# Spreading a kernel's weight transfers over more of the run, and splitting one more input weight ahead

## The chip, the cores and the metric

The kernel runs on one core of a Trainium2 chip. Its time is the device time of one execution in microseconds (us). A core has five engines that run their own queues of instructions and wait for each other by semaphores: TensorE (PE, matrix products), VectorE (DVE), ScalarE (ACT), GpSimd (POOL) and SyncE (SP). Here POOL and SP issue the DMA transfers: SP loads, POOL most stores and everything that adds while it moves. All transfers run on 16 DMA engines.

## What is computed

One decoder layer on x of 2048 rows by 1024 columns, in fp32:

```python
h = x * (1.0 + sc1) + sh1
z = h @ w_in[l]
gate_b, gate_c, v_conv, v_pool = jnp.split(z, [CONV_CH, 2 * CONV_CH, 3 * CONV_CH], axis=-1)
y_conv = gate_b * _short_conv(gate_c * v_conv, conv_w[l])
y_pool = _multiscale_pool(v_pool, w_pool[l], pool_scale[l])
mix = jnp.concatenate([y_conv, y_pool], axis=-1) @ w_out[l]
x = _layer_norm(DEEPNORM_ALPHA * x + (1.0 + g1) * mix, ln1_g[l], ln1_b[l])
h = x * (1.0 + sc2) + sh2
f = jnp.square(jax.nn.relu(h @ w_mlp_in[l])) @ w_mlp_out[l]
x = _layer_norm(DEEPNORM_ALPHA * x + (1.0 + g2) * f, ln2_g[l], ln2_b[l])
```

w_in is 1024 x 2048, w_out 1024 x 1024, w_mlp_in 1024 x 4096, w_mlp_out 4096 x 1024; the shifts, scales and gates come from a conditioning vector and w_ada.

## The kernel before

**Products.** The rows are worked in two blocks of 1024. Each fp32 operand is split into a high half (fp32r, a cast on ACT, line 145) and a low half (the rest, a subtraction on DVE, line 146); a product of 128 x 128 by 128 x 512 is then three matmuls, high by high, high by low and low by high (`mm3`, lines 152, 153 and 154). The large products use seven products of halved blocks in place of eight (a Strassen scheme), so that sums of weight blocks and of operand blocks are needed. `seven` (line 626) runs one such set of seven: a product takes a pair (high, low) of a weight from the list `made`, or splits one, runs 8 `mm3` (24 matmuls), and splits the next weight behind itself. The split weights live in six tiles `w` of 128 x 1024, that is three pairs. The names of the operand blocks in their order are 11, 12, s2, s1, s3, s4, 22 for the weights and "11", "21", "2", "1", "3", "22", "4" for the inputs.

**Stages on PE, in order.** Block 0: input projection (`in_proj_0`, to about 190 us), output projection (`out_proj`, to about 270), first map of the MLP (`first_map`, eight groups of seven products, 448 `mm3`, to about 580). Block 1: input projection (`in_proj_1`, four groups of seven products, 224 `mm3`, to about 735), output projection (112 `mm3`, to about 819), first map (448 `mm3`, to about 1131). Then the second map (`down`, 26 products, to 1701) and the last normalisation. During the first map of a block, each group's results are squared on ACT, added in many combinations on DVE (`sums`, quarter tiles of 128 x 256) and stored to the DRAM tensor `usum` by POOL (line 1108). The last group of block 0 leaves these sums `owed`; `flush` hands them out inside block 1's input projection.

**The weight transfers.** The second map needs sums of blocks of w_mlp_out. They are not worked on DVE: `sums_down` (line 1187) is a list of 20 sums of 4 parts each, 80 DMA transfers of 512 KB from DRAM to DRAM into `wsum`, all issued by POOL at line 1191; 40 of them copy, 40 add into what is there. They are handed out one at a time: once the generator `sums_down()` is in the list `beside_products`, each `mm3` counts one beat, and at the beats of the set `W_BEATS` (line 31) one transfer is issued; `behind` lets POOL wait for that `mm3`'s last matmul. POOL's queue is in order, so what stands behind a transfer there (stores of `usum`, of `msum`, loads of x) waits as well. Before the change the list is filled after block 0's first map, so that beat 1 is the first `mm3` of block 1's input projection: beats 56 to 206 (26 of them) lie in that projection, beats 207 to 359, with its end and the output projection, have none, and 54 transfers follow from beat 360 on, every seventh beat, in block 1's first map; the last at beat 731 of 784.

**The turn from block 0 to block 1.** Ahead of product 5 of the last group of block 0's first map, `prepare` (line 716) is called: it starts the generator of the projection's weights (`summed_weights`, line 620: an SP load into one of five tiles `r`), splits the first weight, and makes the inputs "11", "21" and "2" (`inputs`, line 694: two SP loads each; the first two kinds are scaled and shifted on ACT, "2" is only split). `in_proj_1` (line 724) then runs group 0; behind its first product it splits the second weight, flushes one owed stage and makes input "1"; behind the second product it splits the third weight, adds, flushes the rest and makes input "3"; and so on. At the end of a projection its results are mixed and stored to `msum` (lines 418 and 420, POOL), and the output projection's operands are loaded from `msum`, `gout` and `wosum` by SP (lines 923, 931 and 941). In the last group the pooling (line 334) and the convolution (lines 398 to 400) run between the last products; `keep` (line 731; the copy is line 733) empties PE's banks on ACT.

**What sets the order.** The source gives each instruction its engine and a priority (its place in the program). A planner lays down each engine's queue when the kernel is built, by its own estimate of when an operand or a free tile is there; so an engine's order can differ from the source's, PE's too, and an edit at one place can move instructions at others. On the chip every queue runs in the order so laid down.

Of the kernel before, what the change touches and what calls it, by code (L numbers as in the profile page):

```python
# [27 lines left out]
WINDOWS = (2, 4, 8, 16)  # L28
HALO = 16
Q = 256  # L30
W_BEATS = {*range(56, 210, 6), *range(360, 776, 7)}
QUARTERS = slice(0, 256), slice(256, 512)

SLOTS = 26
# [73 lines left out]
def tile_hybrid_layer(ctx: ExitStack, tc: tile.TileContext, opening, xT, x, wada, win,  # L108
# [26 lines left out]
    def t_r():  # L135
        return mk(big, [P, T], F32, "r", 5)

    def t_ps():
        return mk(pp, [P, H], F32, "ps", 8)
# [11 lines left out]
    def mm3(ps, whi, wlo, xhi, xlo, first, last, goes_on=False):  # L151
# [4 lines left out]
        if beside_products:  # L156
            beats[0] += 1
            if beats[0] in W_BEATS:
                with behind(done.ins):
# [186 lines left out]
    def parts(src, t=t_h):  # L346
        hi, lo = t(), t()
        split(src, hi, lo)
        return hi, lo
# [239 lines left out]
    ORDER = (("11", "11"), ("12", "21"), ("s2", "2"), ("s1", "1"), ("s3", "3"), ("s4", "22"), ("22", "4"))  # L589
# [33 lines left out]
            nc.sync.dma_start(r, src[i] if i in RAW else sums[i - 4])  # L623
            yield r

    def seven(ready, B, first_w=None):
        made = [first_w] if first_w else []

        def product(i, banks, new):
            hi, lo = made.pop() if made else parts(next(ready), t_w)  # L630
            for p in range(2):
                if new:
                    banks[p] = t_ps()
                for k in range(4):
                    bh, bl = B[ORDER[i][1], k // 2]
                    ks = slice((k % 2) * H, (k % 2) * H + H)
                    cs = slice(p * H + k * P, p * H + k * P + P)
                    mm3(banks[p], hi[:, cs], lo[:, cs], bh[:, ks], bl[:, ks], new and k == 0, k == 3,
                        not new)
            for r in ready:  # L640
                made.append(parts(r, t_w))
                break

        return product
# [49 lines left out]
    def inputs(X, key):  # L694
        for q in range(2):
            r = t_r()
            X[key, q] = hi, lo = t_h(), t_h()
            if len(key) == 1:
                src, hs = xsum[(int(key) + 1) % 2], halves[int(key) % 4 > 0 and int(key) < 3]
                k = 2 * q  # L700
            else:
                k, hs = 4 * int(key[0]) - 4 + 2 * q, halves[int(key[1]) - 1]
                src = xT
            nc.sync.dma_start(r.rearrange("p (a n) -> p a n", a=2),
                              src[k : k + 2, :, hs].rearrange("a p n -> p a n"))
            if len(key) == 1:
                split(r, hi, lo)
                continue
            for dst in (hi, r):
                for a, cs in enumerate(halves):  # L710
                    nc.scalar.activation(dst[:, cs], r[:, cs], AF.Identity,
                                         bias=mod[:, 2 * (k + a) + SH1 : 2 * (k + a) + SH1 + 1],
                                         scale=mod[:, 2 * (k + a) + SC1 : 2 * (k + a) + SC1 + 1])
            tt(lo, r, hi.bitcast(F32), ALU.subtract)

    def prepare():
        X = {}
        W = summed_weights(wins[0], winsum, (0, 1, 5, 4, 6, 7, 3))
        first_w = parts(next(W), t_w)
        for i in range(3):  # L720
            inputs(X, ORDER[i][1])
        return X, W, first_w

    def in_proj_1(X, W, first_w):
        mixed = []
        ops = Operands(mixed)

        def cut(rows_, h):
            return [r[:, o + h * H : o + h * H + H] for r, o in rows_]

        def keep(dst, banks):
            for p in range(2):
                nc.scalar.copy(dst[p], banks[p])  # L733

        def add(dst, banks):
            for p in range(2):
                tt(dst[p], dst[p], banks[p], ALU.add)

        def group(j):
            x_, y_, z_ = {}, {}, {}  # L740
            ready = W if j == 0 else block_weights(wins[j])
            product = seven(ready, X, None if j else first_w)
            v, u = t_o(WW), t_o(WW)
            values = (v, HALO), (u, 2)
            product(0, x_, True)
            keep(cut(values, 0), x_)
            if owed:
                flush(1)
            nc.vector.tensor_copy(v[:, :HALO], vhalo[:, j, :])
            nc.vector.tensor_copy(u[:, :2], uhalo[:, j, :])  # L750
            if j == 0:
                inputs(X, ORDER[3][1])
            product(1, y_, True)
            add(cut(values, 0), y_)
            flush()
            if j == 0:
                inputs(X, ORDER[4][1])
            yield
            gc, gb = t_o(), t_o()
            gates = (gc, 0), (gb, 0)  # L760
            last = j == NG - 1
            product(2, x_, False)
            keep(cut(values, 1), x_)
            if j == 0:
                inputs(X, ORDER[5][1])
            product(3, z_, True)
            keep(cut(gates, 1), z_)
            if j == 0:
                inputs(X, ORDER[6][1])
            if last:  # L770
                ops.begin(0)
            yield
            product(4, x_, False)
            add(cut(gates, 1), x_)
            if last:
                ops.begin(1)
            product(5, z_, False)
            add(cut(values, 1), z_)
            if last:
                ops.weights(0, 1)  # L780
                pt = pool_mid(1, j, v)
            product(6, x_, False)
            keep(cut(gates, 0), x_)
            if last:
                ops.weights(1, 1)
                ops.second(0)
            yield
            if not last:
                pt = pool_mid(1, j, v)
            y = gc  # L790
            for hs in halves if last else [slice(0, T)]:
                w = hs.stop - hs.start
                tt(u[:, 2 + hs.start : 2 + hs.stop], u[:, 2 + hs.start : 2 + hs.stop], gc[:, hs], ALU.mult)
                conv(j, u[:, hs.start : hs.stop + 2], y[:, hs], w)
                tt(y[:, hs], y[:, hs], gb[:, hs], ALU.mult)
                if last and hs.start == 0:
                    mixed.extend([y[:, :H], None, pt[:, :H], pt[:, H:]])
                    ops.third(0)
                    ops.third(1)
            sums = mixed_sums(y, pt, u, v)  # L800
            if last:
                mixed[1] = sums[0]
                mixed.extend(sums[1:])
            else:
                store_mixed(j, y, pt, u, v)

        groups = [group(j) for j in range(NG)]
        for _ in range(3):
            next(groups[0])

        for j in range(1, NG):
            last = j == NG - 1
            next(groups[j])
            if not last:
                next(groups[j])
            next(groups[j - 1], None)
            if last:
                next(groups[j])
            next(groups[j])
        next(groups[-1], None)  # L820
        return ops
# [365 lines left out]
    def sums_down():  # L1187
        for kind, to, i in W_SUMS:
            for gp in range(4):
                src = w2[i, gp] if i < 8 else wsum[i - 8, gp]  # L1190
                nc.gpsimd.dma_start(wsum[to - 8, gp], src, max_dma_last_dim=2 * T,  # L1191
                                    accum_op=ALU.add if kind else ALU.bypass)
                yield
# [273 lines left out]
    def first_map(b, B, back):  # L1467
        side = second_side() if b else first_side()
        open_ = []

        def beside(ins):
            if open_:
                with behind(ins):
                    next(side, None)

        def turn():
            if b + 1 < NB:
                ready.append(prepare())

        ups = [up(b, g, B, beside, turn) for g in range(NC)]  # L1480
        for g in range(2):
            next(ups[g])
            back(1 + g)
        for i in range(3, 7):
            next(ups[0])
            back(i)
        open_.append(True)
        for g in range(NC):
            for _ in ups[g]:
                pass  # L1490

    ready = []
    for b in range(NB):
        B, back = out_proj(b, in_proj_1(*ready[0]) if b else in_proj_0())
        first_map(b, B, back)
        if b == 0:
            beside_products.append(sums_down())
    for _ in beside_products.pop():
        pass
    down(gate[0], Close())  # L1500
# [56 lines left out]
```

## Time and profile before

| | |
|---|---|
| time, median of 3 runs | 1710.18 us (1709.5 to 1710.49) |
| the profiled execution | 1709.94 us, of which the span of the trace is 1708.1 |
| PE busy | 1689.0 us |
| DVE, ACT, POOL busy | 1399.6, 844.0, 378.0 us |
| moved by DMA | 469.47 MB, 275 GB/s |

A line of the profile names the line of the kernel, the engine, the operation, and out<-in by the program's names. An arrow <- behind an idle time names what ended it. In the windows, each engine's busy time stands with the count of its instructions, then the granted share of TensorE's clock, the busy share of the DMA engines and GB/s. In the DMA lists stand the count, the size and the median time from issue to landing; in a chain, the start, the duration and what ran.

### The profile page before, as it was taken

What the parts mean: (1) busy time and instruction counts of PE and PEld (TensorE: products, weight loads), DVE (VectorE), ACT (ScalarE), POOL (GpSimd) and SP (SyncE); (2) the same over time, 40 slices, a digit from 0 to 9 for tenths busy, and PEclk for the clock granted to TensorE, in tenths of its full rate; (3) what the DMA queues carried; (4) which work ended last, traced back from release to release, by engine and by line L of the source; (5) the groups of instructions that cost most, each with busy time, mean ns of one, the idle gap of its engine ahead of it and who ended that gap; (6) DMA issues with size and microseconds to landing.
All of it is one profiled execution on the core that took longest, in us unless ns stands there. A gap on an engine that the chain in (4) does not pass through costs nothing.

```text
span 1708.1 us, 22023 instructions
## 1 busy us (share of the span) xinstructions
PE 1689.0 (99%) x7519; PEld 1397.1 (82%) x7519; DVE 1399.6 (82%) x2138; ACT 844.0 (49%) x1160; POOL 378.0 (22%) x687
## 2 busy tenths in 40 slices
PE   9999999999999999999999999999999999999998
PEld 8888888888888778878888887878888888888886
DVE  8898697898897776887888778676988887897898
ACT  6323358555544843446855444455543433334555
POOL 0222221344453312200155445540000000000000
PEclk9999999999999999999999999999999999999999
DMA  9998867657765769975899999999999999886782
GB/s 386 345 337 321 311 253 274 192 194 234 234 220 162 238 216 230 248 259 206 277 279 265 277 265 263 270 316 367 327 332 340 366 338 344 294 337 224 262 292 99
DMA packets 149217, 469.47 MB, mean 275 GB/s; under 512 B 20456, under 2 KB 20976, under 8 KB 149104
## 3 DMA queue, kind: packets, MB, share of 16 engines
q1 hardware_dynamic: 93184, 303.38, 50.0%
q0 software_dynamic: 55920, 164.67, 32.4%
q8 instruction: 59, 0.97, 0.2%
q14 instruction: 54, 0.44, 0.1%
HBM read 350.01 MB, written 159.91 MB: 299 GB/s over the span
## 4 chain that ended last, share of the span: by engine, by line
PE 81%; DMA 7%; DVE 5%; issue 4%; ACT 1%; POOL 1%; SPq 0%; DVEq 0%; POOLq 0%; ACTq 0%
PE ps L152 26%; PE ps L154 26%; PE ps L153 26%; DMA usum<-o 4%; DVE o L163 3%; PE ps L487 3%; PE ps L862 1%; DVE w L146 1%; DMA msum<-o 1%; DMA w<-in_w 1%; DMA r<-in_xT 1%; DMA r<-in_w 0%; POOL wsum L1191 0%; DMA r<-wosum 0%; DVE r L163 0%
## 5 line engine op out<-in xcount | busy, mean ns | idle before, releaser
L154 PE MATMUL ps<-h,w 128*128 128x512 f32 x1312 | 511.0, 390 | 3.6 <-DVE w L146 3.6
L152 PE MATMUL ps<-h,w 128*128 128x512 f32 x1312 | 510.9, 390 | 2.3 <-ACT w L145 1.4
L153 PE MATMUL ps<-h,w 128*128 128x512 f32 x1312 | 510.8, 389 | 0.0
L152 PE MATMUL ps<-h,h 128*128 128x512 f32 (+1 forms) x1064 | 413.5, 389 | 3.0 <-ACT o L733 2.1
L153 PE MATMUL ps<-h,h 128*128 128x512 f32 (+1 forms) x1064 | 413.1, 388 | 1.6 <-DVE h L146 1.6
L154 PE MATMUL ps<-h,h 128*128 128x512 f32 (+1 forms) x1064 | 413.4, 389 | 0.0
L154 PEld LDWEIGHTS ps<-h,w 128*128 128x128 f32 x1312 | 246.3, 188 | 57.3 <-DVE w L146 5.9
L152 PEld LDWEIGHTS ps<-h,w 128*128 128x128 f32 x1312 | 246.2, 188 | 54.7 <-ACT w L145 1.9
L153 PEld LDWEIGHTS ps<-h,w 128*128 128x128 f32 x1312 | 246.3, 188 | 50.8
L1108 POOL DMA_DIRECT2D usum<-o x416 | 224.6, 546 | 279.8 <-DVE o L163 169.2
L145 ACT CAST w<-r 128x1024 fp32r<-128x1024 f32 x156 | 163.9, 1051 | 180.1 <-PE ps L153 172.0
L145 ACT CAST h<-r 128x1024 fp32r<-128x1024 f32 (+1 forms) x136 | 136.5, 1008 | 218.3 <-PE ps L153 93.1
L146 DVE TENSOR_TENSOR w<-r,w 128x1024 fp32r<-128x1024 f32 x156 | 190.2, 1221 | 64.0 <-ACT w L145 62.8
L152 PEld LDWEIGHTS ps<-h,h 128*128 128x128 f32 x1064 | 200.2, 188 | 44.7 <-ACT o L733 2.5
L153 PEld LDWEIGHTS ps<-h,h 128*128 128x128 f32 x1064 | 200.3, 188 | 42.9 <-DVE h L146 2.1
L154 PEld LDWEIGHTS ps<-h,h 128*128 128x128 f32 x1064 | 200.1, 188 | 40.9
L163 DVE TENSOR_TENSOR o<-o,o 128x256 f32<-128x256 f32 (+2 forms) x458 | 200.5, 487 | 11.1 <-DMA usum<-o 7.9
L146 DVE TENSOR_TENSOR h<-r,h 128x1024 fp32r<-128x1024 f32 (+1 forms) x136 | 157.7, 1166 | 62.1 <-ACT h L145 61.9
L145 ACT CAST h<-w 128x1024 fp32r<-128x1024 f32 x104 | 109.0, 1048 | 92.9 <-DVE w L163 84.7
L163 DVE TENSOR_TENSOR o<-o,ps 128x512 f32<-128x512 f32 x184 | 122.5, 682 | 22.8 <-PE ps L154 20.9
L146 DVE TENSOR_TENSOR h<-w,h 128x1024 fp32r<-128x1024 f32 x104 | 126.8, 1220 | 14.6 <-ACT h L145 14.4
L163 DVE TENSOR_TENSOR o<-o 128x256 f32<-128x256 f32 (+1 forms) x176 | 82.1, 469 | 17.5 <-ACT o L1096 8.0
(166 smaller groups left out, 1424.1 us busy)
## 6 DMA issues: line engine op xcount, KB each, us to landing
usum<-o POOLq DMA_DIRECT2D x416, 128.0 KB, 5.6
r<-usum SPq DMA_DIRECT2D x104, 512.0 KB, 5.6
w<-wsum SPq DMA_DIRECT2D x76, 512.0 KB, 7.2
w<-in_w SPq DMA_DIRECT2D x72, 512.0 KB, 6.7
r<-in_w SPq DMA_DIRECT2D x68, 512.0 KB, 6.3
wsum<-in_w POOLq DMA_DIRECT2D x56, 512.0 KB, 9.0
wsum<-wsum POOLq DMA_DIRECT2D x24, 512.0 KB, 6.3
msum<-o POOLq DMA_DIRECT2D x18, 512.0 KB, 6.7
```

The source lines that it names most:

```text
L145: high = nc.scalar.copy(hi, src)
L146: return high.ins, nc.vector.tensor_tensor(lo, src, hi.bitcast(F32), op=ALU.subtract).ins
L152: nc.tensor.matmul(ps, whi, xhi, start=first, stop=False, skip_group_check=goes_on)
L153: nc.tensor.matmul(ps, whi, xlo, start=False, stop=False, skip_group_check=goes_on)
L154: done = nc.tensor.matmul(ps, wlo, xhi, start=False, stop=last, skip_group_check=goes_on)
L163: return nc.vector.tensor_tensor(out_, a, b_, op=op)
L487: nc.tensor.matmul(ps[m, h], wt[:, w : w + P], A[k][p // 2][:, hs], start=k == 0 and p == 0, stop=k == KD - 1 and p == 2)
L862: nc.tensor.transpose(ps[:, t * P : t * P + P], R[4 * h + t][:, k * P : k * P + P], ident)
L1108: nc.gpsimd.dma_start(usum[slot, g // 2, :, b, g % 2, :], z)
```

## The change

Three edits.

1. The list of transfers is opened ahead of block 0's first map, so that its `mm3` count as beats 1 to 448, the input projection's as 449 to 672, the output projection's as 673 to 784 and block 1's first map's as 785 to 1232.
2. The beats are chosen anew: 16 single ones in block 0's first map (44 to 395), 22 in the input projection (498 to 624, every sixth), 42 in block 1's first map (808 to 1218, every tenth).
3. `prepare` splits two weights of the projection and not one, the second between the inputs "21" and "2", and `seven` takes a list of split weights, first in, first out.

```diff
-W_BEATS = {*range(56, 210, 6), *range(360, 776, 7)}
+W_BEATS = {44, 62, 79, 109, 123, 166, 209, 282, 291, 327, 338, 348, 369, 377, 386, 395,
+           *range(498, 628, 6), *range(808, 1224, 10)}
...
-    def seven(ready, B, first_w=None):
-        made = [first_w] if first_w else []
+    def seven(ready, B, first_w=()):
+        made = list(first_w)
 
         def product(i, banks, new):
-            hi, lo = made.pop() if made else parts(next(ready), t_w)
+            hi, lo = made.pop(0) if made else parts(next(ready), t_w)
...
     def prepare():
         X = {}
         W = summed_weights(wins[0], winsum, (0, 1, 5, 4, 6, 7, 3))
-        first_w = parts(next(W), t_w)
-        for i in range(3):
+        first_w = [parts(next(W), t_w)]
+        for i in range(2):
             inputs(X, ORDER[i][1])
+        first_w.append(parts(next(W), t_w))
+        inputs(X, ORDER[2][1])
         return X, W, first_w
...
-            product = seven(ready, X, None if j else first_w)
+            product = seven(ready, X, () if j else first_w)
...
         B, back = out_proj(b, in_proj_1(*ready[0]) if b else in_proj_0())
-        first_map(b, B, back)
         if b == 0:
             beside_products.append(sums_down())
+        first_map(b, B, back)
```

## Prediction

> **What bounds the kernel now.** I read the busy shares first, then who TensorE waited for, then the place of each wait, then the chain behind the large ones.
>
> ```profile
> PE 1689.0 (99%) x7519; PEld 1397.1 (82%) x7519; DVE 1399.6 (82%) x2138; ACT 844.0 (49%) x1160; POOL 378.0 (22%) x687
> ```
>
> TensorE (PE) is busy for 1689.0 of 1708.1 us. No matmul is added or removed, so the change can only take away or add idle time of PE. All that there is of it (engine, line waited for: total us, times, longest):
>
> ```profile
> PE ps L154 <- DVE w L146: 3.6, 4, 1.3
> PE ps L152 <- ACT o L733: 2.1, 1, 2.1
> PE ps L153 <- DVE h L146: 1.6, 1, 1.6
> PE ps L152 <- ACT w L145: 1.4, 1, 1.4
> PE ps L192 <- DVE o L194: 1.1, 1, 1.1
> PE ps L152 <- DVE h L163: 0.9, 1, 0.9
> PE ps L152 <- ACT o L1083: 0.8, 1, 0.8
> PE ps L487 <- DVE h L458: 0.2, 1, 0.2
> ```
>
> Together 11.7 us in eleven places; 1.1 + 0.2 lie at the opening and 0.9 at the end, out of the change's reach. The timeline of PE gives the places (start, duration, then the idle time before it):
>
> ```profile
> 361.94 0.50 PE L154 MATMUL ps<-h,w 128*128 128x512 f32 x1 [0.52 <-DVE w L146]
> 575.84 0.50 PE L152 MATMUL ps<-h,w 128*128 128x512 f32 x1 [1.44 <-ACT w L145]
> 599.54 0.50 PE L154 MATMUL ps<-h,w 128*128 128x512 f32 x1 [1.19 <-DVE w L146]
> 746.59 0.50 PE L152 MATMUL ps<-h,h 128*128 128x512 f32 x1 [2.11 <-ACT o L733]
> 987.42 0.50 PE L154 MATMUL ps<-h,w 128*128 128x512 f32 x1 [0.62 <-DVE w L146]
> 1027.15 0.51 PE L154 MATMUL ps<-h,w 128*128 128x512 f32 x1 [1.32 <-DVE w L146]
> 1115.06 0.50 PE L152 MATMUL ps<-h,w 128*128 128x512 f32 x1 [0.84 <-ACT o L1083]
> 1144.42 0.50 PE L153 MATMUL ps<-h,h 128*128 128x512 f32 x1 [1.64 <-DVE h L146]
> ```
>
> By stage: 361.94 is in block 0's first map, 575.84 and 599.54 where block 1's input projection begins, 746.59 at its output projection, 987.42 to 1115.06 in block 1's first map, 1144.42 at the start of the second map. The windows show the clock and the DMA load (PE, PEld, DVE, ACT, POOL busy, then granted clock, DMA share, GB/s):
>
> ```profile
> 747.20:750.60 3.40, 3.40 (x10) 2.62 (x9) 3.40 (x5) 1.13 (x3) 1.05 (x2) 0.50 0.79 231
> 284.00:574.00 290.00, 289.48 (x1278) 239.16 (x1277) 239.12 (x405) 168.06 (x201) 116.66 (x218) 1.00 0.63 203
> 833.00:1100.00 267.00, 265.06 (x1167) 217.98 (x1166) 215.56 (x374) 137.29 (x165) 131.17 (x222) 1.00 0.99 265
> ```
>
> Right behind the 2.11 us gap the clock is 0.50 for 3.4 us: 1.70 us more is lost there, so that place costs 3.81. Block 0's first map runs with the DMA engines 0.63 busy, block 1's with 0.99: that is where the 54 transfers of the second range lie.
>
> **The change, part by part.**
>
> *(a) The transfers leave the end of the input projection.* The old last beats there are 182 to 206, the new last one is 624 - 448 = 176. The old beat 176 is the issue at 702.62; the five issues behind it go, of which the first and the last are shown:
>
> ```profile
> 702.62 0.93 POOL L1191 DMA_DIRECT2D wsum<-in_w  x1 [3.53 <-PE ps L154]
> 706.70 0.88 POOL L1191 DMA_DIRECT2D wsum<-in_w  x1 [3.15 <-PE ps L154]
> ...
> 723.02 0.57 POOL L1191 DMA_DIRECT2D wsum<-wsum  x1 [3.48 <-PE ps L154]
> ...
> 717.25 14.03 DMA msum<-o
> 732.15 6.05 DMA r<-wosum
> 744.73 1.33 ACT o L398 x2
> 746.07 0.48 ACT o L733
> ```
>
> The last four rows are from the chain that ends in the 746.59 gap: a store of msum, issued between those transfers, takes 14.03 us to land; SP's load of it, the wosum loads queued behind, ACT's casts and DVE's subtractions follow; DVE reaches the convolution late, ACT's two L398 wait for it, and the copy L733 that empties PE's bank stands behind them. In the input projection before that, at the same queue:
>
> ```profile
> msum<-o POOLq DMA_DIRECT2D x6, 512.0 KB, 6.7
> ```
>
> At 6.7 instead of 14.03 the chain starts 7.3 us earlier; 2.11 are needed. Bounds: nothing (something else on the chain is as late) to -3.81. I take **-3.81**, since 7.3 is over three times the need. Late next is DVE's queue at 741 to 744, which the same wait holds.
>
> *(b) Block 1's first map gets 42 transfers at every tenth beat instead of 54 at every seventh.* Two gaps end a chain with a usum store (128 KB) in it; below them the median landing of such stores in 290 to 420 (block 0's first map) and in 980 to 1132:
>
> ```profile
> 972.70 12.00 DMA usum<-o
> 1011.79 12.65 DMA usum<-o
> ...
> usum<-o POOLq DMA_DIRECT2D x81, 128.0 KB, 3.8
> usum<-o POOLq DMA_DIRECT2D x103, 128.0 KB, 7.2
> ```
>
> DVE overwrites the stored tiles only when the store has landed, and its next weight's low half waits in line. The excess is 12.00 - 3.8 = 8.2 us and more; with 30% fewer transfers per time 2.5 us of it go, against gaps of 0.62 and 1.32. Bounds 0 to -1.94; I take **-1.94**.
>
> *(c) The second weight is split ahead.* `made` now always holds one pair more, so the fourth weight of the projection is split in front of DVE's owed sums and the halves of the operand "3" and not behind them. DVE's row for it, and what is ahead of it:
>
> ```profile
> 594.33 1.22 DVE L146 TENSOR_TENSOR h<-r,h 128x1024 fp32r<-128x1024 f32 x1
> ...
> 596.47 1.22 DVE L146 TENSOR_TENSOR h<-r,h 128x1024 fp32r<-128x1024 f32 x1
> ...
> 598.27 1.22 DVE L146 TENSOR_TENSOR w<-r,w 128x1024 fp32r<-128x1024 f32 x1
> ```
>
> PE takes it at 599.54. The two "3" halves alone are 2 x 1.22 = 2.44 us, twice the gap; they are wanted a product later, 24 matmuls x 0.2265 us (289.48 / 1278 above) = 5.4 us. Bounds 0 to -1.19; I take **-1.19**.
>
> The price of (c): SP loads that weight ahead of two loads of "2" instead of behind them, and the split takes a pair of the six `w` tiles. With the first weight, the second and the map's product 5 the three pairs are full, and product 6's split, which has waited for product 4's pair, waits for product 5's last matmul. PE has the projection's first product (5.4 us) to run meanwhile. If the order doesn't put it there, a cast and a subtraction, about 1.05 + 1.22 us, stand open in place of the 1.44 at 575.84. Bounds: -1.44 to +2.3 - 1.44 + 1.70 (a clock drop) = +2.5; I take **0**, the middle and the case that this first product hides it.
>
> *(d) Sixteen transfers go into block 0's first map.* It is a third of the other map's old density (16 over 351 beats, 54 over 371). The cost is on its usum stores: a third of 7.2 - 3.8 is 1.1 us on a store. The gap at 361.94 has one store and one weight load in its chain, behind a stretch in which DVE is full; I add the 1.1 there: **+1.1**. Bounds: 0 (hidden in DVE's 290 - 239 = 51 idle us) to one pair like 0.62 + 1.32 in each of seven groups, +13.6.
>
> *(e) The last transfers.* New beats 384 to 434 of that map against old ones to 395. But the old queue ran late: its last two issues are these, and the chain to 1144.42 has this load:
>
> ```profile
> 1096.91 0.95 POOL L1191 DMA_DIRECT2D wsum<-in_w  x1 [2.71 <-DMA wsum<-in_w]
> 1113.05 0.94 POOL L1191 DMA_DIRECT2D wsum<-in_w  x1 [0.83 <-DMA usum<-o]
> ...
> 1120.99 10.36 DMA w<-in_w
> ```
>
> Beat 434 is 39 beats x 0.68 us, 26 us, behind 395: some four transfers then meet the second map's first loads instead of one or two. Bounds -0.84 (the gap at 1115.06 goes) to +2.5 (as in c); I take **0**.
>
> The sum is -3.81 - 1.94 - 1.19 + 0 + 1.1 + 0 = -5.84. The profiled execution took 1709.94 (span 1708.1 and 1.8 around it), the median of the runs shown is 1710.18; from the median: **1704.3 us**.
>
> **The clock rule.** The half clock in 747.20:750.60 follows 2.11 us of idling; behind the 1.64 us gap at 1144.42 the window keeps 1.00:
>
> ```profile
> 1140.00:1160.00 20.00, 18.36 (x82) 14.87 (x81) 16.82 (x22) 7.73 (x8) 4.56 (x9) 1.00 1.03 344
> ```
>
> The Trainium skill, "TensorE: Matmul & The Clock Gate", says in "Why this matters for your kernels" that gaps up to about 3 us don't drop the clock, and in Part 1 that the monitor's window is 3413 ns. The trace agrees with the window's length (3.4 us at 0.50), not with the limit. By the page (a) would be worth 2.11 and the time 1706.0.
>
> **The rivals.**
> 1. *The thinning does nothing.* POOL's issues come in bunches behind its stores, as 1096.91 and 1113.05 show, not at the beats. Then (b) is 0 and the time 1710.18 - 3.81 - 1.19 + 1.1 = 1706.3. For it: the shares of 0.99 leave a backlog that survives. Against: fewer transfers are also smaller bunches. 0.20, with the rule's 1706.0 in it (0.03).
> 2. *DVE's queue takes the place of the msum store.* The order on the engines is laid anew by the planner, ACT and DVE each run theirs in one queue, and another late cast opens a like gap there or at 575.84. Then (a) gives nothing: 1710.18 - 1.94 - 1.19 + 1.1 = 1708.2, no difference. 0.24.
> 3. *Slower: block 0's first map becomes the other one.* Each of the sixteen issues stands in POOL's one queue ahead of usum stores, and DVE, 239.12 of 290 us busy there, waits for their tiles; POOL carries loads of x too. If each of seven groups then shows 1.94 of gaps, the time is 1710.18 - 6.94 + 13.6 = 1716.8. It decides from 6.94 / 7 = 0.99 us a group, and is measurably slower from 1.48. The Trainium skill, "DMA: Bandwidth & Descriptors", section "Issuing engines are not separate DMA queues", speaks for it: SP's loads and POOL's transfers share the same 16 engines. Against: 0.63 of share leaves room for a third of the density that brought the other to 0.99. 0.18.
>
> **How the numbers follow.** A measurement of this kernel tells about 0.2%, 3.4 us, from no change. The forecast has 0.38, rival 1 0.20 (both faster: 0.58), rival 2 0.24 (same), rival 3 0.18 (slower). The low end is the forecast with (d) at 0, (e) at -0.84 and the 1.44 gone: 1704.3 - 1.1 - 0.84 - 1.44 = 1700.9, say 1701. The high end takes rivals 1 and 2 and half of rival 3 (up to three or four groups with gaps, 1710.18 - 6.94 + 5 x 1.94 = 1712.9): 1713. Some 0.1 is left out on each side.
>
> **What would show it.** (a): no PE gap at the first out-projection product, the clock 1.00 there, msum stores landing in 7 to 9 us. (b): usum stores in block 1's first map under 10 us, its DMA share near 0.9. (c): the fourth weight's low half at least 5 us ahead of its matmul, and product 6's split behind product 5. (d): usum landings there near 5 us, no gap over 1.6. The prediction is wrong if a gap over 2 us with a half clock stands anywhere new, or if the gaps of the first map of block 0 add up to more than 3 us.

## The result and the profile after

The changed kernel takes **1706.52 us** (median of 15 runs) against 1710.18 (15 runs): ratio 0.9981 [0.9973, 0.9989], 3.7 us less where 5.84 were forecast. Measured once more on another chip, beside the experiments, it was 0.9994 [0.9986, 1.0003], some 1 us less, which can't be told from none. (The brackets are 95% intervals of the ratio.) The profiled execution took 1707.25 us (span 1705.5, before 1708.1).

Who TensorE waited for, in the changed kernel (line numbers are 1 to 3 higher than before):

```profile
PE ps L153 <- ACT w L146: 4.2, 1, 4.2
PE ps L153 <- ACT o L1086: 1.7, 1, 1.7
...
PE ps L154 <- DVE h L147: 0.9, 1, 0.9
...
PE ps L155 <- DVE w L147: 0.5, 2, 0.3
```

The four waits for a weight's low half have shrunk to two short ones, the 2.1 us for L733 are gone, and one wait of 4.2 us for a weight's cast is new. The timeline of PE says where:

```profile
361.36 0.50 PE L155 MATMUL ps<-h,w 128*128 128x512 f32 x1 [0.24 <-DVE w L147]
564.36 0.50 PE L153 MATMUL ps<-h,w 128*128 128x512 f32 x1 [1.65 <-ACT o L1086]
581.84 0.80 PE L153 MATMUL ps<-h,w 128*128 128x512 f32 x1 [4.23 <-ACT w L146]
```

The gaps of before at 599.54, 746.59, 987.42, 1027.15 and 1115.06 have no counterpart. Both long ones stand at the turn from block 0 to block 1, where before had 1.44: the 1.65 at product 4 of block 0's last group, the 4.23 at its product 6. The wait at the start of the second map is 0.90 us (before 1.64). The first matmul behind the 4.23 takes 0.80 us and not 0.50, since the clock is at half there; the windows of the turn, of the output projection's beginning and of the two first maps:

```profile
580.86:587.69 6.83, 5.85 (x14) 4.65 (x15) 5.90 (x8) 1.88 (x2) 2.24 (x5) 0.50 0.92 263
746.00:750.00 4.00, 4.00 (x20) 3.30 (x19) 4.00 (x6) 1.62 (x3) 1.06 (x2) 1.00 0.78 227
284.00:574.00 290.00, 288.11 (x1268) 237.30 (x1267) 234.77 (x401) 162.26 (x193) 128.97 (x234) 1.00 0.74 229
833.00:1100.00 267.00, 266.75 (x1185) 220.32 (x1184) 219.95 (x381) 140.11 (x167) 124.73 (x217) 1.00 0.88 244
```

The output projection begins without idling at full clock. Block 1's first map went from a DMA share of 0.99 to 0.88 and lost its idle time (266.75 of 267 busy, before 265.06). Block 0's went from 0.63 to 0.74 and lost 1.37 us of PE's work (289.48 to 288.11), which is the gap at 564.36 for the one at 361.94.

Why, the chain to the second gap shows (start, duration, what ran):

```profile
548.73 10.96 DMA r<-in_xT
559.72 0.82 ACT h L712
560.53 0.95 ACT o L1098
...
579.89 0.95 ACT h L146
580.84 0.96 ACT w L146
581.84 0.80 PE ps L153
```

It begins with SP's first load of block 1's x. ScalarE's queue is in order: the scaling of x (L712), the squares owed by the last group (L1098, L1099), the copies that empty PE's banks (L1086) and the casts of the weights stand in one line behind that load, and the cast that ends last is that of block 0's product 6. Before, the same chain began with these two steps:

```profile
549.09 5.17 DMA r<-in_xT
...
554.28 0.82 ACT h L711
```

The load was issued at the same time and took half as long; everything behind it is 5.4 us later now (559.72 - 554.28). What lies beside it, by the DMA share (last column but one) before:

```profile
540.00:544.00 4.00, 4.00 (x19) 3.33 (x18) 4.00 (x13) 2.63 (x4) 3.33 (x7) 1.00 0.37 131
544.00:548.00 4.00, 4.00 (x20) 3.30 (x19) 4.00 (x11) 2.03 (x3) 3.53 (x7) 1.00 0.74 252
548.00:552.00 4.00, 4.00 (x19) 3.33 (x18) 2.33 (x4) 0.10 (x2) 1.70 (x4) 1.00 1.01 217
552.00:556.00 4.00, 4.00 (x19) 3.31 (x18) 1.92 (x2) 2.77 (x4) 0.00 (x0) 1.00 0.64 206
```

and in the changed kernel, with two of the sixteen transfers on POOL's timeline:

```profile
540.00:544.00 4.00, 4.00 (x20) 3.30 (x19) 4.00 (x14) 2.91 (x4) 3.73 (x7) 1.00 0.97 214
544.00:548.00 4.00, 4.00 (x19) 3.34 (x18) 4.00 (x10) 1.83 (x3) 2.76 (x6) 1.00 1.10 227
548.00:552.00 4.00, 4.00 (x19) 3.30 (x19) 2.04 (x5) 0.36 (x1) 3.10 (x5) 1.00 0.89 227
552.00:556.00 4.00, 4.00 (x20) 3.30 (x19) 1.85 (x2) 0.69 (x1) 0.00 (x0) 1.00 0.97 189
556.00:560.00 4.00, 4.00 (x19) 3.34 (x18) 0.00 (x0) 0.28 (x1) 0.00 (x0) 1.00 0.84 307
...
537.41 0.98 POOL L1194 DMA_DIRECT2D wsum<-in_w  x1
548.05 0.94 POOL L1194 DMA_DIRECT2D wsum<-in_w  x1 [0.19 <-issue]
```

The DMA engines are 0.84 to 1.10 busy from 540 to the moment at which x lands, where before had 0.37 to 1.01. The share alone doesn't make the place, though. Before has stretches as full elsewhere in that map; this is one of them, and below it is one of the sixteen transfers of the changed kernel, which falls into it:

```profile
392.00:396.00 4.00, 4.00 (x19) 3.34 (x18) 4.00 (x10) 1.87 (x3) 3.52 (x8) 1.00 1.08 226
...
394.60 0.97 POOL L1194 DMA_DIRECT2D wsum<-in_w  x1
```

In the changed kernel PE has no gap over 0.1 us between 362 and 564. What sets the turn apart is the load of x, on which ScalarE's whole queue hangs, and that PE waited at the end of this chain already (1.44 us): there was no slack.

### The profile page after: what moved, and what is told of

Same layout as the page of the kernel before. It is cut to its first block, busy times and chain, and to the rows that moved or that the text cites. A ratio compares the mean times of both kernels' runs of the same rounds, so it can differ in the third digit from the quotient of the medians.

```text
span 1705.5 us, 22025 instructions
## 1 busy us (share of the span) xinstructions
PE 1688.1 (99%) x7519; PEld 1396.8 (82%) x7519; DVE 1399.6 (82%) x2138; ACT 844.2 (49%) x1160; POOL 377.9 (22%) x687
## 4 chain that ended last, share of the span: by engine, by line
PE 90%; DVE 4%; DMA 3%; ACT 1%; issue 1%; POOL 0%; DVEq 0%; SPq 0%; ACTq 0%; POOLq 0%
PE ps L153 29%; PE ps L155 29%; PE ps L154 29%; PE ps L488 3%; DVE o L164 2%; DMA r<-in_xT 1%; PE ps L865 1%; DMA usum<-o 1%; DVE w L147 1%; DMA w<-in_w 1%; DVE r L164 0%; DMA wsum<-in_w 0%; DMA r<-in_w 0%; POOL usum L1111 0%; ACT w L146 0%
```

## The experiments

**Theory L** (late load): the transfers that are under way when the load of x starts make it late. **Rival O** (order): the second weight's split, which stands ahead of product 6's cast in ScalarE's queue and needs a free pair of `w`, makes it late. Each profile is one execution, and the 15 timed executions of before lie between 1706.54 and 1712.36 us; so gaps are read from the profiles and gains from the timed ratios, all against the kernel before on the same chip. In the expectations, "the first SiLU" is the scaling of x (L712), "the two-set projection" is block 1's input projection, and the gap "before its second product" is the one of 4.23 us.

**The beats alone** (before, with the new beats and the earlier opening of the list, one split ahead):

```diff
-W_BEATS = {*range(56, 210, 6), *range(360, 776, 7)}
+W_BEATS = {44, 62, 79, 109, 123, 166, 209, 282, 291, 327, 338, 348, 369, 377, 386, 395,
+           *range(498, 628, 6), *range(808, 1224, 10)}
...
-        first_map(b, B, back)
         if b == 0:
             beside_products.append(sums_down())
+        first_map(b, B, back)
```

> The new beats and the earlier opening of the list, with the old single split ahead. In the changed kernel PE loses some 7.5 us at the turn to block 1: gaps of 1.65 at 562.71 and 4.23 at 577.61 and a half clock behind the second. Theory L (the load): the sixteenth transfer, at beat 395, makes a load of x for block 1 land in 10.96 us instead of 5.2, and ACT's queue stands behind it; then this kernel keeps both gaps (about 1.6 and 4) and gets back the 1.19 at the projection's fourth product: 1.2 to 1.5 us slower than the changed kernel, ratio to before about 0.999. Rival O (the order): the second weight's cast ahead of product 6's, and its tiles, make the 4.23; then that gap goes back to about 1.4 without a clock drop, some 5.7 us, and the kernel is about 4 us faster than the changed one, ratio about 0.9955.

1706.78 us, ratio 1.0002 [0.9993, 1.001]. **The split alone** (before, with the hunks of `seven`, `prepare` and `product` of the change):

> The old beats, with two weights split ahead. Theory L: the load of x lands in about 5 us, the gap before product 6 stays at 1.4 to 1.7, the gap at the projection's fourth product goes, the one at 746 with its half clock and those at 987 and 1027 stay: 1.2 to 1.5 us faster than before, ratio about 0.9992. Rival O: a gap of about 4 us with a half clock at the turn: about 4 us slower than before, ratio about 1.0025.

1704.93 us, ratio 0.9996 [0.9984, 1.0007]. The gap at 599 is gone, as expected; but those at 987 and 1027 are gone too, and the one at the output projection (1.88 us) has no half clock behind it, against the expectation. **The second split later** (the changed kernel, `prepare` as before, and the second weight split in `in_proj_1` ahead of product 0):

```diff
             product = seven(ready, X, () if j else first_w)
+            if j == 0:
+                first_w.append(parts(next(W), t_w))
```

> The changed kernel with the second weight's load and split not in the preparation but at the beginning of the input projection, behind product 6's split; still two are split ahead from there. Theory L: ACT is as late as before by the load, gaps of about 1.6 and 4 stay, the fourth product's gap stays away: within 0.5 us of the changed kernel, ratio about 0.998. Rival O: the gap before product 6 goes back to about 1.4 without a clock drop: 5 to 6 us faster than the changed kernel, ratio about 0.9947.

1705.99 us, ratio 1.0 [0.9991, 1.0008]. PE's rows at product 6, of these three in turn:

```profile
578.31 0.79 PE L153 MATMUL ps<-h,w 128*128 128x512 f32 x1 [4.67 <-ACT w L146]
```

```profile
576.78 0.50 PE L152 MATMUL ps<-h,w 128*128 128x512 f32 x1 [0.82 <-ACT w L145]
```

```profile
578.51 0.53 PE L153 MATMUL ps<-h,w 128*128 128x512 f32 x1 [4.64 <-ACT w L146]
```

The gap goes with the beats and not with the split: both kernels with the new beats and one split ahead have it, the one with old beats and two splits has not. Rival O falls. Two of the three timed ratios (1.0002 and 1.0) are above what L had given (0.999 and 0.998), so its sizes were not right yet.

**The last transfer of the map earlier** (the changed kernel, beat 235 for beat 395):

```diff
-W_BEATS = {44, 62, 79, 109, 123, 166, 209, 282, 291, 327, 338, 348, 369, 377, 386, 395,
+W_BEATS = {44, 62, 79, 109, 123, 166, 209, 235, 282, 291, 327, 338, 348, 369, 377, 386,
```

> The changed kernel with one beat of the sixteen moved: 235 in place of 395, so that nothing is issued behind beat 386. Theory L: the load of x lands in 5 to 7 us, the gap at 562 goes and the one before product 6 falls to 1.4 to 2 without a clock drop: 5 to 7.5 us faster than the changed kernel, ratio to before about 0.994 to 0.995. Rival O: only the gap at 562 goes, 1.65 to 2 us: ratio about 0.997.

1704.23 us, ratio 0.9985 [0.9977, 0.9994]; the forecast of .994 to .995 was missed. The load of x still took long, and the gap is smaller but there:

```profile
551.12 7.33 DMA r<-in_xT
```

```profile
580.47 0.50 PE L153 MATMUL ps<-h,w 128*128 128x512 f32 x1 [2.79 <-ACT w L146]
```

Here the last transfer starts at 539.8 us and has landed at 546.3, before the load begins. So no large transfer has to be under way beside the load; the run with one more at the turn, below, shows what was in flight instead. The moved transfer cost something as well: block 0's first map, up to 537 us, has a new gap of 1.22 us at 477.87.

**The turn cleared** (the changed kernel, the last three of the sixteen moved into the in-projection):

```diff
-W_BEATS = {44, 62, 79, 109, 123, 166, 209, 282, 291, 327, 338, 348, 369, 377, 386, 395,
-           *range(498, 628, 6), *range(808, 1224, 10)}
+W_BEATS = {44, 62, 79, 109, 123, 166, 209, 282, 291, 327, 338, 348, 369,
+           *range(498, 623, 5), *range(808, 1224, 10)}
```

> The changed kernel, with the three transfers of beats 377, 386 and 395 taken out of block 0's first map (13 stay, the last at about 527 us) and put among those beside block 1's in-projection (25, every 5th beat from 498, the last at about 705 us). Theory L (the transfers at 537 and 548 us make the load of x at 548.7 us late, ScalarE queues behind it): the first SiLU of the next block starts near 554.3 us and not at 559.7, the gap at 564.36 (1.65) is gone, the gap before the second product of the two-set projection is 0.8 to 1.5 us instead of 4.23, no half clock there; time about 7 us under the changed kernel's, ratio to the kernel before .993 to .996. Rival M (the turn is slower because all sixteen transfers shift the first map, or because the second weight's split stands ahead of the sixth's casts): the gap of about 4 us and the half clock stay, ratio .998 to 1.000.

**The changed kernel once more**, on the same chip:

> The changed kernel once more, beside the other three. Theory L: the load of x that starts near 548.7 us takes about 9 to 11 us again, the gap before the second product of the two-set projection is 4 to 5 us again with the half clock, ratio .9975 to .9995. Rival (the long load was a chance of one execution): load of 5 us, gap under 2 us, same ratio.

1700.13 us, ratio **0.9966** [0.9953, 0.998], against 1704.42, 0.9994 [0.9986, 1.0003]: the intervals do not overlap. The load of x, ScalarE's first step behind it and PE's gap with the turn cleared:

```profile
548.62 5.59 DMA r<-in_xT
```

```profile
554.24 0.82 ACT L712 ACTIVATE h<-r,mod 128x512 fp32r<-128x512 f32 x1 [1.66 <-DMA r<-in_xT]
```

```profile
576.15 0.50 PE L153 MATMUL ps<-h,w 128*128 128x512 f32 x1 [0.64 <-ACT w L146]
```

and the last two in the repetition of the changed kernel:

```profile
558.44 0.82 ACT L712 ACTIVATE h<-r,mod 128x512 fp32r<-128x512 f32 x1 [5.66 <-DMA r<-in_xT]
```

```profile
580.34 0.80 PE L153 MATMUL ps<-h,w 128*128 128x512 f32 x1 [4.04 <-ACT w L146]
```

L holds: with the three transfers away the step starts at the old time, the gap and the half clock are gone, and the kernel beats both others. Its gain over the changed kernel, 4.3 us, is smaller than the expected 7: in the repetition the changed kernel has 0.28 and not 1.65 us at product 4, and a half clock half as long.

**The last one moved** (beat 395 goes to 492, 386 stays):

```diff
-W_BEATS = {44, 62, 79, 109, 123, 166, 209, 282, 291, 327, 338, 348, 369, 377, 386, 395,
-           *range(498, 628, 6), *range(808, 1224, 10)}
+W_BEATS = {44, 62, 79, 109, 123, 166, 209, 282, 291, 327, 338, 348, 369, 377, 386,
+           *range(492, 628, 6), *range(808, 1224, 10)}
```

> The changed kernel with the one transfer of beat 395 (548 us) moved to the in-projection (beat 492); that of beat 386 (537 us) stays. If the transfer that starts with the load of x alone makes it late: the first SiLU near 554.5 us, no gap of more than 1.5 us at the turn, no half clock, ratio .996 to .998, as with all three moved. Rival (the transfers at 531 and 537 us still fill the queues): the load takes 7 us or more, gap 2 to 4 us, ratio .998 to 1.000.

1701.09 us, ratio 0.9979 [0.997, 0.9987]. ScalarE starts at 555.03; the gap is 1.82 us, and the half clock still falls behind it:

```profile
577.35 0.50 PE L153 MATMUL ps<-h,w 128*128 128x512 f32 x1 [1.82 <-ACT w L146]
```

```profile
577.70:581.10 3.40, 3.40 (x10) 2.62 (x9) 3.40 (x5) 0.54 (x1) 1.08 (x2) 0.50 0.98 230
```

The one transfer was most of it, not all; the expectation of no gap over 1.5 us and no half clock was missed. The window of the turn gives its size, in the changed kernel and with the last one moved:

```profile
536.00:560.00 24.00, 24.00 (x107) 19.88 (x106) 15.85 (x33) 9.06 (x12) 11.92 (x21) 1.00 0.91 226
```

```profile
536.00:560.00 24.00, 24.00 (x108) 19.87 (x107) 17.04 (x35) 13.63 (x18) 12.15 (x23) 1.00 0.79 205
```

(0.91 - 0.79) x 24 = **2.9 us of all sixteen engines for one transfer**, an estimate from two single profiles. With all three moved the share is 0.62, as it was before.

**One more at the turn** (beat 391 added, 498 taken out):

```diff
-W_BEATS = {44, 62, 79, 109, 123, 166, 209, 282, 291, 327, 338, 348, 369, 377, 386, 395,
-           *range(498, 628, 6), *range(808, 1224, 10)}
+W_BEATS = {44, 62, 79, 109, 123, 166, 209, 282, 291, 327, 338, 348, 369, 377, 386, 391, 395,
+           *range(504, 628, 6), *range(808, 1224, 10)}
```

> The changed kernel with a seventeenth transfer beside block 0's first map, at beat 391 (542 to 546 us), and one fewer in the in-projection: the suspected cost doubled. Theory L: the load of x near 548.7 us lands later than at 559.7, the first SiLU near 562 us or later, the gaps before the two-set projection's first and second product add to 7 us or more (5.88 in the changed kernel), ratio 1.001 to 1.004. Rival (the loads wait for something else): the same gaps and ratio as the changed kernel beside its repetition, .9985 to 1.0005.

1703.59 us, ratio 0.9989 [0.9979, 0.9999], 0.46 and 4.02 us of gaps at the two places against 0.28 and 4.04 in the repetition of the changed kernel. Its timeline, with the added transfer, a store behind it and the next transfer:

```profile
541.35 1.00 POOL L1194 DMA_DIRECT2D wsum<-in_w  x1
548.86 0.54 POOL L1111 DMA_DIRECT2D usum<-o  x1 [1.25 <-DMA wsum<-in_w]
554.58 0.57 POOL L1194 DMA_DIRECT2D wsum<-wsum  x1
...
580.66 0.79 PE L153 MATMUL ps<-h,w 128*128 128x512 f32 x1 [4.02 <-ACT w L146]
```

This expectation was wrong, but the edit didn't double what it was to double: the transfer of beat 395 now came out of POOL's queue at 554.58, behind the load of x, and the added one took its place at 541. The number issued ahead of the load was the same, and so was the result.

The run says more about how the load becomes late. The transfer of 541.35 had landed at 548.33, before the load of x began at 548.98, and the load took 9.76 us even so. What was in flight are a weight load and stores of `usum`: POOL issues these in one queue with the transfers, and the row at 548.86 shows one that waited for a transfer to land. The `usum` stores issued between 542 and 549 us, with their median time to landing, in before, with the last transfer earlier, and here:

```profile
usum<-o POOLq DMA_DIRECT2D x12, 128.0 KB, 2.4
...
usum<-o POOLq DMA_DIRECT2D x11, 128.0 KB, 4.4
...
usum<-o POOLq DMA_DIRECT2D x8, 128.0 KB, 8.3
```

With the turn cleared it is 2.3 us, with the last one moved 5.4. So the load is late with a transfer beside it, and also behind one, with late stores beside it. That it is the late stores that hold it there is argued; no run separates the two.

**The projection's end cleared** (before, term (a) alone):

```diff
-W_BEATS = {*range(56, 210, 6), *range(360, 776, 7)}
+W_BEATS = {*range(56, 186, 5), *range(360, 776, 7)}
```

> The kernel before, with its 26 transfers beside block 1's in-projection made every 5th beat instead of every 6th, so that the last starts at about 706 us instead of 723; all others as before. Term (a) alone. Theory (the transfers at 711 to 723 us delay the sums' store): no gap at the first product of the output projection (746.59, 2.11 us) and no half clock at 747.2 to 750.6; 2 to 4 us less, ratio .9977 to .999. Rival (the store is late for another reason): the gap of about 2 us stays, ratio 1.000.

**The kernel before once more**:

> The kernel before once more. If the gaps at 599.54, 987.42 and 1027.15 us belong to the places of the weight transfers and to the single split, they stand there again; the rival (they come and go from one execution to the next, as the run that only moved the second split has none at 987 and 1027 with the same places) has one or more of the three gone or elsewhere. The gap at 746.59 is expected to stand in either case. Ratio 1.000.

With the end cleared 1702.9 us, ratio 0.9979 [0.9968, 0.9989], 3.6 us (1.9 to 5.5); no gap at the output projection's first product. The repetition of before took 1705.43, ratio 1.0 [0.9989, 1.0011]; its stores of msum in 700 to 735 us, its longest gap behind the turn, and the clock there:

```profile
msum<-o POOLq DMA_DIRECT2D x3, 512.0 KB, 12.9
```

```profile
743.67 0.50 PE L152 MATMUL ps<-h,h 128*128 128x512 f32 x1 [1.30 <-ACT o L733]
```

```profile
743.67:747.07 3.40, 3.40 (x15) 2.83 (x16) 3.40 (x5) 0.52 (x1) 1.14 (x3) 1.00 0.85 255
```

The gap at the output projection stands again, smaller and without the half clock; those at 361, 987 and 1027 do not, of the one at 599 only 0.12 us are left (at 597.12), and one of 1.23 us at 907.38 is there instead. With the end cleared the same stores land sooner:

```profile
msum<-o POOLq DMA_DIRECT2D x3, 512.0 KB, 7.1
```

**The second map denser** (the cleared kernel with `range(808, 1102, 7)`, term (b) taken back):

> As the run with the turn cleared (13, 25 and 42 transfers), but the 42 beside block 1's first map every 7th beat from 808 to 1095, as dense as in the kernel before. Term (b) alone, taken back. If thinning is worth 1.9 us (theory of the prediction): ratio .0011 above that run's, and gaps of 0.6 to 1.3 us at block 1's first map (990 to 1030 us). Rival (those gaps come and go and thinning does nothing): the same ratio as that run within the interval, .996 to .998, waits of one chunk no longer than there.

1700.29 us, ratio 0.9973 [0.9964, 0.9983]. **A single split** (the cleared kernel's beats, `seven` and `prepare` of before, term (c) taken back):

> As the run with the turn cleared, with the kernel before's single weight split ahead: the beats alone. Term (c) taken back. If the second split ahead is worth 1.2 us: ratio .0007 above that run's, with a gap of about 1 us near 599 us. Rival (that gap comes and goes; order at the turn is neutral): the same ratio within the interval, .996 to .997, the gap before the second product of the two-set projection 1.0 to 1.5 us.

1700.75 us, ratio 0.9977 [0.9966, 0.9987]. Both stand 0.0007 to 0.0011 above the cleared kernel's 0.9966, where the theories had 0.0011 and 0.0007, but the intervals overlap: the times leave (b) and (c) open. The denser run has no gap at 990 to 1030 us, but one of 1.26 at 878.96; the single split has 0.59 at 599.17, where about 1 was expected.

A single profile doesn't settle them either, but the fourteen together say more. All kernels run 7519 matmuls; the start of the matmul with the same number, less its start in the repetition of before, grows from one place to the next by (us; the first column counts from the opening, and the sum goes to the second map's end, so that it can hold a little more than the columns). The repetition itself is the row of zeros that is left out.

| profile | 1st map to 537 | turn to 594 | to 607 | to 741 | out-proj. start | block 1's map | 2nd map's start | sum |
|---|---|---|---|---|---|---|---|---|
| before, first chip | 0.9 | 0.5 | 1.0 | -0.3 | 2.4 | 1.0 | 1.0 | 6.5 |
| split alone | 0.9 | -0.1 | -0.5 | 0.8 | 0.6 | -0.5 | 1.3 | 2.6 |
| projection's end cleared | 0.9 | 0.1 | 0.4 | -0.1 | -1.6 | -1.1 | 0.6 | -0.8 |
| changed kernel, first chip | 0.5 | **8.0** | -0.5 | -0.3 | -1.6 | -1.3 | -0.9 | 3.9 |
| changed kernel once more | 0.6 | **5.1** | -0.5 | -0.3 | -1.6 | -1.5 | -1.4 | 0.5 |
| beats alone | -0.3 | **6.1** | 0.0 | -0.3 | -1.6 | -1.9 | -1.2 | 0.9 |
| second split later | 0.4 | **5.3** | -0.5 | -0.3 | -1.6 | -2.0 | -1.4 | -0.1 |
| last beat earlier | 2.6 | **3.4** | -0.5 | -0.3 | -1.6 | -1.6 | -0.8 | 1.8 |
| one more at the turn | 0.8 | **5.2** | -0.5 | -0.3 | -1.6 | -1.9 | -0.6 | 1.2 |
| last one moved | 0.4 | 2.5 | -0.5 | -0.3 | -1.6 | -1.7 | -1.6 | -2.7 |
| turn cleared | 0.4 | -0.3 | -0.5 | 0.2 | -1.6 | -1.0 | -0.6 | -3.3 |
| second map denser | -0.4 | 0.8 | -0.5 | 0.5 | -1.6 | 0.3 | -2.1 | -2.9 |
| single split | 1.1 | 0.5 | 0.4 | -0.3 | -1.6 | -1.9 | -1.5 | -3.3 |

Block 1's map: the five profiles with seven beats between transfers (the first three, the repetition at 0.0, the denser one) average -0.1 (-1.1 to 1.0), the nine with ten beats -1.6 (-2.0 to -1.0). But the one direct pair, denser and cleared, gives it back: 1.3 us more in the map, 1.5 less at the second map's start, where the denser kernel's last transfers lie earlier. The second split: 0.4 in the mean of the five with one split, -0.5 in all others, in its own column, and given back in part two products later (0.8, 0.2, 0.5 where the turn is clear).

## Why the prediction was right and wrong

The time came out inside the range, 2.2 us above the forecast, but not by the mechanism that was forecast. The prediction named its own sign of being wrong, a gap over 2 us with a half clock anywhere new, and that gap is there: 4.23 us at 581.84. By the table's first and fourth rows, the turn lost 7.5 us (8.0 against 0.5), and the other places together gained 10.1, where the terms other than (d) forecast 6.94. That the two left 2.6 between the profiled executions, near enough to the forecast, was luck. The parts, between these two executions:

- **(a), -3.81: right.** The stores land in 7.3 us (13.7 before), the output projection starts without a gap at full clock, and the place gives 4.0. Alone it is worth 3.6 us by the times. Its size there has chance in it: the repetition of before idles 1.30 us at that place with no half clock, and the place gives 1.6 us against it.
- **(b), -1.94: the size about right, the reading weak.** The median usum store fell from 7.2 to 5.6 us (6.5 in the repetition of the changed kernel), the share from 0.99 to 0.88. But the two gaps it was read from are not the place's own: they come and go between executions. The 1.5 us of the fourteen profiles speak for the thinning, inside the map; the direct pair gives as much back at the second map's start, and the times don't settle it.
- **(c), -1.19: at most some 0.7.** In the first pair of profiles the 599.54 gap goes; over all of them the gain in its column is some 0.9, and with the next column, where part comes back, 0.7 (0.3 where the turn is clear). The times show none. Its price, put at 0, was right: the split alone has 0.82 at product 6, not more than 1.44.
- **(d), +1.1: the step that failed.** "The cost is on its usum stores", the prediction says of the sixteen, and of the gap at 361.94: "I add the 1.1 there". At that place the gap fell to 0.24, and the stores there land in 4.4 us where before had 3.8. The price stood at the turn, which the term didn't look at: some 7.4 us in this pair (4.23 + 1.65 for 1.44, and 2.9 of half clock), 5.1 to 5.4 on the second chip (the repetition of the changed kernel against that of before, and against the turn cleared). The sixteen were weighed by their mean density and charged to the small stores; what decides is which load a single one meets. The rows of before that tell it were in the trace: the chain to the 575.84 gap begins with the load of x at 549.09 and ends in a wait of PE, so a later load goes into PE's time (5.4 us later here, and 4.4 us more of gaps), and beat 395 of 448 can be laid on it. I read the map's mean of 0.63 instead. The same prediction allowed the turn up to +2.5 under (c), for the split; the split wasn't the cause, as the run with the split alone shows.
- **(e), 0: a gain that was put at nothing.** The second map's start is 1.9 us faster in the first pair, beyond the bound of -0.84, and faster in all profiles with the list opened earlier (-0.6 to -2.1) than in those without (0.0 to 1.3). The wait of before at 1115.06 came from ScalarE's queue, held 10 us by a load of usum (1109.44 in before); in the changed kernel that load holds it 6.4 us (10.10 and 5.48 in the two repetitions):

```profile
1109.44 1.05 ACT L145 CAST h<-r 128x1024 fp32r<-128x1024 f32 x1 [10.19 <-DMA r<-usum]
```

```profile
1104.90 1.05 ACT L146 CAST h<-r 128x1024 fp32r<-128x1024 f32 x1 [6.40 <-DMA r<-usum]
```

  I had counted transfers that meet the second map's loads, not those that meet this load of `usum`. That the earlier transfers leave a backlog there is argued, not tested.

One bound was not worked as said: the high end speaks of three or four groups with gaps and takes five, 1712.9; with four it would be 1711.0. The result lies inside either.

Of the rivals, the second came nearest in form: a late cast opens a gap at the place of the 575.84. But it made the planner's order the cause, with (a) giving nothing, and both were wrong. The third had the right resource, the engines that SP and POOL share, and the wrong place: the rest of block 0's map shows no systematic loss (0.5 and 0.6 in the changed kernel's two profiles, 0.9 and 0.0 in before's; 2.6 with the beat at 235). The Trainium skill, "DMA: Bandwidth & Descriptors", section "Issuing engines are not separate DMA queues", states that transfers of different issuers run interleaved on the same sixteen engines; the trace agrees, 10.96 us for SP's load beside POOL's transfers against 5.17.

What stays open: why the changed kernel was 0.9981 on one chip and 0.9994 on the other. The chance of the half clock, present at (a) in one profile of before and absent in the other, and twice as long at the turn in one profile of the changed kernel as in the other, would make such differences; that is argued, not shown.

## What to carry to other kernels

Background transfers are priced one by one, at the place where each falls. A mean DMA share over a stage (0.63) doesn't name the place, and a full window doesn't either: the one at 392 to 396 us (1.08) took a transfer without a wait of PE. What named it here is a chain that already ended in a gap of PE and began with a load on which an in-order queue hangs. So list these loads, and lay on the timeline each transfer issued in the twelve microseconds ahead of one, with the stores that wait behind it. And before a gap under 2 us is put into a sum, take a second profile of the unchanged kernel: here four of the eight were gone or nearly so.

## What the runs showed of the hardware

- A DRAM-to-DRAM transfer of 512 KB into `wsum` holds all sixteen DMA engines for some 2.9 us, the estimate worked out above. The first load of block 1's x, of the same size, took 5.2 to 5.6 us from issue to landing in the seven profiles with no transfer issued in the 15 us ahead of it, 6.4 and 7.3 where the last had landed 4 to 5 us ahead (the last one moved, the last beat earlier), 9.0 to 11.0 in the four where one was under way, and 9.8 in the run with one more at the turn, where one had landed 0.65 us ahead and the next came while the load ran.
- The half clock doesn't go by the length of a gap alone. It followed gaps of 4.67, 4.64, 4.23, 4.04, 4.02, 2.79, 2.11 and 1.82 us, and not gaps of 1.97, 1.88 and 1.73 us. It lasted 3.41 us, or twice that behind 4.23 and 4.67. The place on a grid decides: within each of the fourteen traces the changes of the clock, from the first rise to full, lie whole multiples of 3.413 us apart (in the changed kernel full from 4.01, half from 580.86, full from 587.69: 169 and 2 times). With the gaps laid on that grid, every stretch of 3.413 us at full clock that the half clock followed held at least 1.82 us of idling of PE, and no other held more than 1.73: the gaps of 1.97 and 1.88 lie across a line of the grid, as 1.26 + 0.72 and 0.30 + 1.58. The half clock stayed for a second stretch where its first held 0.98 and 2.59 us of idling, and not at 0.50 or less. The Trainium skill, "TensorE: Matmul & The Clock Gate", section "What's actually happening", describes a window of 3413 ns that runs free of the kernel; the lengths and the grid agree. For the prediction's clock rule this means that the 1.70 us behind the 2.11 us gap was the luck of its place.
